# Four load buffers, earlier weights and row sums two ahead in a dilated convolution that runs at the pace of its transfers

## The chip, the cores and the metric

One core of a Trainium2 chip. The metric is the device time of one execution in microseconds (us). Runs marked slow are left out of every comparison, and the medians below are of the fast runs. A ratio is the mean time of one kernel's fast runs over the mean of the other's fast runs of the same rounds, so it isn't quite the ratio of the medians that are quoted. A span, where one is given, is the time from the first to the last instruction in the trace; the measured time is some 2 us longer. The granted clock is the share of its full clock at which TensorE was allowed to run.

## The reference

A 3x3 convolution with dilation 2, 64 channels in, 128 out, on 16 images of 64x64, all f32:

```python
batch, c_in, h, w, c_out, k, dilation = 16, 64, 64, 64, 128, 3, 2
x_pad = np.pad(x, ((0, 0), (0, 0), (pad, pad), (pad, pad)), mode='constant')
# for every b, co, ci, kh, kw:
output[b, co] += weight[co, ci, kh, kw] * x_pad[b, ci, kh*dilation:kh*dilation+h, kw*dilation:kw*dilation+w]
```

The input is 16.8 MB, the output 33.6 MB. Each byte is moved once: 50.63 MB with the weights.

## The kernel before

Images go in eight pairs (two images fill 128 partitions), each pair in four groups of 16 rows. ScalarE casts a group's rows to f16 (`cast`), VectorE adds pairs of rows (`rowsum`), TensorE multiplies into psP, psA and psB, ScalarE copies psP out (`p_sb`), and VectorE adds it to psA and psB while it evicts them (`evac`). The parts that matter here, with cuts:

```python
x32pool = ctx.enter_context(tc.tile_pool(name="x32pool", bufs=3))   # f32 pairs, filled by loads
xpool = ctx.enter_context(tc.tile_pool(name="xpool", bufs=3))       # f16 pairs, filled by casts
opool = ctx.enter_context(tc.tile_pool(name="opool", bufs=3))       # f32 output pairs
...
nc.sync.dma_start(out=w32, in_=weight.rearrange("o i h w -> o (i h w)"))
for pb in range(min(3, npairs)):
    load(pb, first[pb])
...
for i in range(14):                                     # dummies on TensorE
    nc.tensor.matmul(out=wp[:, 0:512], lhsT=warm[:, 0:P], rhs=warm)
...                                                     # weight differences wd
cast(0)
...
rowsum(0)
...                                                     # transposes wt, copies w_sb
def prepare(n):
    n = min(n, ngroups)
    while ahead[1] < min(n - 1 if n < ngroups else n, ahead[0]):
        rowsum(ahead[1]); ahead[1] += 1
    while ahead[0] < n:
        cast(ahead[0]); ahead[0] += 1

for G in range(ngroups):
    ...                                                 # products into psP, psA, psB; p_sb <- psP
    evac(0, psA)
    prepare(min(G + 3 + G // 3, G + 1 + LOOK))
    evac(1, psB)
    if ahead[0] >= NG * (freed[0] + 1) and freed[0] + 3 < npairs:
        load(freed[0] + 3, [H])                         # waits until the oldest f32 pair is cast
        freed[0] += 1
    ...                                                 # stores: pairs 0 and 7 in halves, others whole
```

Loads and stores are issued by SyncE, in this order, on one queue.

## Time and profile before

| | before |
|---|---|
| time, median of the first three runs | 133.54 us (132.32 to 134.15) |
| span of the profiled run (134.03 us) | 131.3 us |
| bytes moved | 50.63 MB |
| DMA rate where the queue is full | 428 GB/s |
| last eviction ends | 116.6 us |

The prediction below shows the lines. They are read from the DMA row: a digit is the busy share of the 16 DMA engines in a fortieth of the span, and the GB/s row tells whether busy engines also moved their bytes at the usual rate. A line of windows has, from left to right: from and to (us), the length, the busy us (and number of instructions) of TensorE, of its weight loads, of VectorE, ScalarE and GpSimd, then the granted clock, the DMA share and the GB/s. A DMA share near 1 means that all 16 engines are busy (it can read a little over 1, since a packet is counted where it starts).

The profiled run of 134.03 us is marked slow in its result file. Its span, 131.3 us, lies inside that of the fast runs of the same kernel (129.8 to 132.2), so the profile is used here.

### The profile page before, as it was taken

How to read it: one execution, taken by the hardware profiler on the slowest of the kernel's cores; microseconds unless marked ns; L12 is line 12 of the kernel's file. 1: busy time of each engine (PE TensorE's matmuls, PEld its weight loads, DVE VectorE, ACT ScalarE, POOL GpSimd, SP SyncE). 2: the span in 40 equal slices, each digit the busy share in tenths (PEclk: the TensorE clock that was granted, in tenths of full speed). 3: DMA queues.
4: the chain of work that ended last, by engine and by line, in shares of the span. 5: the costliest groups of instructions: out<-in, count | busy, mean ns of one | idle time of the engine just before them, and what ended most of it. 6: DMA issues, size and time to landing. Idle time of an engine off the chain costs nothing.

```text
span 131.3 us, 2313 instructions
## 1 busy us (share of the span) xinstructions
PE 107.2 (82%) x989; PEld 49.3 (38%) x989; DVE 89.9 (68%) x105; ACT 66.8 (51%) x71; POOL 0.7 (1%) x6
## 2 busy tenths in 40 slices
PE   6906898888999999999999999999999999900000
PEld 2502343333445444544444444444444544400000
DVE  0704466689788888988898889888888987750000
ACT  3536555474696766665565557666766433300000
POOL 2000000000000000000000000000000000000000
PEclk9996799999999999999999999999999999998555
DMA  5999938999999999999999999999999999999960
GB/s 165 399 424 439 424 160 274 359 397 419 429 432 334 369 299 434 424 412 444 424 439 424 422 429 429 434 429 419 429 434 434 414 434 429 429 419 417 429 284 17
DMA packets 4185, 50.76 MB, mean 387 GB/s; under 512 B 464, under 2 KB 464, under 8 KB 592
## 3 DMA queue, kind: packets, MB, share of 16 engines
q1 hardware_dynamic: 4176, 50.63, 93.4%
q8 instruction: 7, 0.11, 0.3%
q14 instruction: 2, 0.02, 0.0%
HBM read 17.07 MB, written 33.55 MB: 385 GB/s over the span
## 4 chain that ended last, share of the span: by engine, by line
PE 64%; DVE 2%; DVEq 1%; ACT 1%; issue 0%
PE psA L164 26%; PE psB L164 24%; PE psP L164 14%; DVE osb L220 2%; DVEq L270 1%; ACT x_266 L87 1%; DVE xs L97 0%; DVEq L220 0%
## 5 line engine op out<-in xcount | busy, mean ns | idle before, releaser
L164 PEld LDWEIGHTS <-w_sb 64*128 64x128 f16 x960 | 46.7, 95 | 61.6 <-DVE xs L97 4.7
L216 ACT COPY p_sb<-psP 128x1024 f32<-128x1024 f32 x32 | 32.4, 1013 | 40.3 <-issue 22.1
L220 DVE TENSOR_TENSOR osb<-psA,p_sb 128x1024 f32<-128x1024 f32 x32 | 39.2, 1225 | 19.2 <-PE psA L164 18.1
L220 DVE TENSOR_TENSOR osb<-psB,p_sb 128x1024 f32<-128x1024 f32 x32 | 39.0, 1218 | 0.0
L164 PE MATMUL psP<-xs,w_sb 64*128 64x496 f16 (+1 forms) x192 | 26.2, 379 | 6.8 <-DVE w_sb L150 4.3
L164 PE MATMUL psA<-x_117,w_sb 64*128 64x496 f16 (+3 forms) x48 | 6.7, 420 | 0.0
L87 ACT CAST x_117<-x_80 128x1024 f16<-128x1024 f32 (+2 forms) x4 | 4.2, 1054 | 3.3 <-DMA x_80<-in_x_dram 3.3
L122 PE MATMUL wp<-warm 128*128 128x512 f16 x14 | 4.7, 510 | 1.2 <-DVE warm L119 1.2
L164 PE MATMUL psB<-x_117,w_sb 64*128 64x496 f16 (+3 forms) x48 | 5.6, 366 | 0.0
L164 PE MATMUL psB<-x_266,w_sb 64*128 64x496 f16 (+3 forms) x48 | 5.6, 365 | 0.0
L164 PE MATMUL psB<-x_392,w_sb 64*128 64x496 f16 (+3 forms) x48 | 5.6, 365 | 0.0
L164 PE MATMUL psB<-x_681,w_sb 64*128 64x496 f16 (+3 forms) x48 | 5.6, 365 | 0.0
L164 PE MATMUL psB<-x_844,w_sb 64*128 64x496 f16 (+3 forms) x48 | 5.6, 365 | 0.0
L164 PE MATMUL psB<-x_518,w_sb 64*128 64x496 f16 (+3 forms) x48 | 5.6, 365 | 0.0
L164 PE MATMUL psB<-x_1166,w_sb 64*128 64x496 f16 (+3 forms) x48 | 5.6, 365 | 0.0
L164 PE MATMUL psA<-x_266,w_sb 64*128 64x496 f16 (+3 forms) x48 | 5.6, 365 | 0.0
L164 PE MATMUL psA<-x_392,w_sb 64*128 64x496 f16 (+3 forms) x48 | 5.6, 365 | 0.0
L164 PE MATMUL psA<-x_681,w_sb 64*128 64x496 f16 (+3 forms) x48 | 5.6, 365 | 0.0
L164 PE MATMUL psA<-x_844,w_sb 64*128 64x496 f16 (+3 forms) x48 | 5.6, 365 | 0.0
L164 PE MATMUL psB<-x_1005,w_sb 64*128 64x496 f16 (+3 forms) x48 | 5.6, 365 | 0.0
L164 PE MATMUL psA<-x_518,w_sb 64*128 64x496 f16 (+3 forms) x48 | 5.6, 365 | 0.0
L164 PE MATMUL psA<-x_1005,w_sb 64*128 64x496 f16 (+3 forms) x48 | 5.6, 365 | 0.0
(34 smaller groups left out, 60.6 us busy)
## 6 DMA issues: line engine op xcount, KB each, us to landing
out_dram<-osb SPq DMA_DIRECT2D x12, 2048.0 KB, 16.6
out_dram<-osb SPq DMA_DIRECT2D x8, 1024.0 KB, 11.1
x_80<-in_x_dram SPq DMA_DIRECT2D x1, 2048.0 KB, 7.6
x_82<-in_x_dram SPq DMA_DIRECT2D x1, 2048.0 KB, 12.0
x_84<-in_x_dram SPq DMA_DIRECT2D x1, 2048.0 KB, 16.5
x_225<-in_x_dram SPq DMA_DIRECT2D x1, 2048.0 KB, 8.5
x_353<-in_x_dram SPq DMA_DIRECT2D x1, 2048.0 KB, 13.0
x_476<-in_x_dram SPq DMA_DIRECT2D x1, 2048.0 KB, 10.6
```

The lines of the kernel that those rows point to most:

```text
L87: nc.scalar.copy(out=x16_tiles[pb][:, lo * W : hi * W], in_=x32_tiles[pb][:, lo * W : hi * W])
L122: nc.tensor.matmul(out=wp[:, 0:512], lhsT=warm[:, 0:P], rhs=warm)
L164: nc.tensor.matmul(out=po, lhsT=w_sb[pp, t * CO : (t + 1) * CO], rhs=rhs, start=first and j == 1, stop=last and j == 2,)
L216: nc.scalar.copy(out=p_sb, in_=psP)
L220: nc.vector.tensor_tensor(out=o[:, :, b0 : b0 + NBLK, e], in0=ps.rearrange("p (m b q) -> p m b q", m=2, q=2 * W), in1=pv, op=add,)
L270: with _tile.TileContext(nc) as tc:
```

## The change

The intent: keep the queue filled from the start (a fourth f32 buffer, paid for with the third f16 one), and let TensorE begin earlier and without gaps (weights ready before the first cast, dummies, products of zeros that nobody reads, so that its clock doesn't drop, row sums two groups ahead). The diff is abridged:

```diff
+    XB = 4
-    x32pool = ... bufs=3
-    xpool = ... bufs=3
+    x32pool = ... bufs=XB
+    xpool = ... bufs=2
-    for pb in range(min(3, npairs)):
-        load(pb, first[pb])
+    for pb in range(min(XB, npairs)):
+        load(pb, [H])
-    wp = apool.tile([P, 1024], f32, tag="ab", name="wp")
+    wp = ppool.tile([P, 1024], f32, tag="p", name="wp")
-    cast(0)
-    rowsum(0)                        (both ahead of the weights' transposes and copies)
+    run_warm(14)                     (14 more dummies, after them)
-    def prepare(n):                  (row sums first, one behind the casts)
+    def prepare(casts, sums):
+        while ahead[0] < min(casts, ngroups):
+            cast(ahead[0])
+            ahead[0] += 1
+        while ahead[1] < min(sums, ngroups):
+            rowsum(ahead[1])
+            ahead[1] += 1
-    prepare(2)
+    prepare(1, 1)
+    prepare(2, 2)
-        prepare(min(G + 3 + G // 3, G + 1 + LOOK))
+        prepare(min(G + 3 + (G + 1) // 2, G + 1 + LOOK), G + 3)
-        ... freed[0] + 3 < npairs: load(freed[0] + 3, [H])
+        ... freed[0] + XB < npairs: load(freed[0] + XB, [H])
```

More of the change, by code (lines that the diff above doesn't have):

```diff
@@ L53 @@
     chunk_rows = [(g * GR + (d if g else 0), min((g + 1) * GR + d, H)) for g in range(NG)]
+    XB = 4
     LOOK = 4
     wpool = ctx.enter_context(tc.tile_pool(name="wpool", bufs=1))
-    x32pool = ctx.enter_context(tc.tile_pool(name="x32pool", bufs=3))
-    xpool = ctx.enter_context(tc.tile_pool(name="xpool", bufs=3))
+    x32pool = ctx.enter_context(tc.tile_pool(name="x32pool", bufs=XB))
+    xpool = ctx.enter_context(tc.tile_pool(name="xpool", bufs=2))
     opool = ctx.enter_context(tc.tile_pool(name="opool", bufs=3))
@@ L109 @@
     nc.sync.dma_start(out=w32, in_=weight.rearrange("o i h w -> o (i h w)"))
-    first = [[H]] * 3
-    for pb in range(min(3, npairs)):
-        load(pb, first[pb])
+    for pb in range(min(XB, npairs)):
+        load(pb, [H])
     ident = wpool.tile([P, P], f16, name="ident")
@@ L119, with run_warm @@
     nc.vector.memset(warm, 0.0)
-    wp = apool.tile([P, 1024], f32, tag="ab", name="wp")
-    for i in range(14):
-        nc.tensor.matmul(out=wp[:, 0:512], lhsT=warm[:, 0:P], rhs=warm)
+    wp = ppool.tile([P, 1024], f32, tag="p", name="wp")
+    def run_warm(n):
+        for _ in range(n):
+            nc.tensor.matmul(out=wp[:, 0:512], lhsT=warm[:, 0:P], rhs=warm)
+    run_warm(14)
     KINDS = 5
@@ L134 @@
         nc.scalar.copy(out=wdv[:, 4, :, r], in_=wv[:, 2])
-    cast(0)
     for r in range(2):
         nc.vector.tensor_tensor(out=wdv[:, 3, :, r], in0=wv[:, 0], in1=wv[:, 1], op=sub)
-    rowsum(0)
     w_sb = wpool.tile([P, KINDS * KW * CO], f16, name="w_sb")
@@ L175, in blocks @@
         return lambda pp, c0, c1: v[pp, b0 : b0 + n, e, :, c0:c1]
-    ahead = [1, 1]
-    def prepare(n):
-        n = min(n, ngroups)
-        while ahead[1] < min(n - 1 if n < ngroups else n, ahead[0]):
+    run_warm(14)
+    ahead = [0, 0]
+    def prepare(casts, sums):
[3 more added lines that the diff above has]
+        while ahead[1] < min(sums, ngroups):
             rowsum(ahead[1])
             ahead[1] += 1
-        while ahead[0] < n:
-            cast(ahead[0])
-            ahead[0] += 1
-    prepare(2)
+    prepare(1, 1)
+    prepare(2, 2)
     freed = [0]
@@ L227 @@
         evac(0, psA)
-        prepare(min(G + 3 + G // 3, G + 1 + LOOK))
+        prepare(min(G + 3 + (G + 1) // 2, G + 1 + LOOK), G + 3)
         evac(1, psB)
-        if ahead[0] >= NG * (freed[0] + 1) and freed[0] + 3 < npairs:
-            load(freed[0] + 3, [H])
+        if ahead[0] >= NG * (freed[0] + 1) and freed[0] + XB < npairs:
+            load(freed[0] + XB, [H])
             freed[0] += 1
```

## The prediction

> **What bounds the kernel now.** I read the page's forty slices first, then the DMA queues, then windows cut where the DMA rows change, then the queue's own waits, and TensorE's timeline for the head. The slices:
>
> ```profile
> PE   6906898888999999999999999999999999900000
> DVE  0704466689788888988898889888888987750000
> PEclk9996799999999999999999999999999999998555
> DMA  5999938999999999999999999999999999999960
> GB/s 165 399 424 439 424 160 274 359 397 419 429 432 334 369 299 434 424 412 444 424 439 424 422 429 429 434 429 419 429 434 434 414 434 429 429 419 417 429 284 17
> ```
>
> TensorE has no work in the last five slices (16 us), VectorE in the last four; the DMA row stays at 9 almost to the end. The chain that ended last names TensorE for 64% of the span, but that chain only explains when the last store was issued: TensorE ends at 115.4 us of 131.3, and what remains is stores that were already queued. So the bound is the DMA queue, and what can be gained is the time in which it did not run at full rate. The windows show that time:
>
> ```profile
> 2.30:17.50 15.20, 10.39 (x69) 4.50 (x69) 6.51 (x12) 7.12 (x11) 0.00 (x0) 0.89 1.02 427
> 17.50:20.00 2.50, 2.26 (x22) 0.87 (x18) 1.40 (x2) 1.62 (x2) 0.00 (x0) 1.00 0.04 13
> 20.00:50.00 30.00, 28.25 (x270) 12.83 (x272) 24.21 (x29) 19.61 (x20) 0.00 (x0) 1.00 0.98 373
> 50.00:126.00 76.00, 65.22 (x634) 30.66 (x630) 57.55 (x63) 37.22 (x38) 0.00 (x0) 0.96 1.01 428
> 126.00:130.00 4.00, 0.00 (x0) 0.00 (x0) 0.00 (x0) 0.00 (x0) 0.00 (x0) 0.50 0.28 117
> ```
>
> The last two columns are DMA share and GB/s. Full rate here is 428 GB/s. There is one real hole, 17.5 to 20.0, and a stretch, 20 to 50, that runs at 373 although its share of busy time is 0.98: packets in it take longer. The last row is the tail, in which the 16 engines finish one after another.
>
> ```profile
> q1 hardware_dynamic: 4176, 50.63, 93.4%
> SPq L78 <- ACT x_117 L87: 10.3, 1, 10.3
> 11.08 1.43 PE L164 MATMUL psP<-xs,w_sb 64*128 64x512 f16 x6 [4.34 <-DVE w_sb L150]
> ...
> 16.42 0.81 PE L164 MATMUL psP<-xs,w_sb 64*128 64x512 f16 x6 [0.47 <-DVE xs L97]
> ```
>
> The first line is the page's (packets, MB, share), the second from the waits of the DMA queue, the others from TensorE's timeline (start, length). The second line gives the cause of the hole: the fourth load is held for 10.3 us until ScalarE has cast the last rows of the first pair (it is issued at 19.14), because there are three f32 buffers; the three loads in flight are done at 17.5, and the first store is not issued before 21.32. The other two show TensorE's head: it waits 4.34 us before its first product, and each of the next groups waits for its row sum.
>
> The time before as a sum of DMA terms: first bytes at 2.2; 50.63 MB at 428 GB/s is 118.3; hole 2.5 x 0.96 = 2.4; slow stretch 30 x (1 - 373/428) = 3.9; together 126.8, which is the mean end of the engines (126 + 4 x 0.28 = 127.1). The last engine is at about 129.9, a tail of 3.0, and the span closes 1.4 later. 2.2 + 118.3 + 2.4 + 3.9 + 3.1 + 1.4 = 131.3.
>
> **What the Trainium skill says.** "DMA: Bandwidth & Descriptors", section "Where 436 GB/s comes from", puts the ceiling of the SBUF side at 435 GB/s; 428 held for 76 us agrees, so the 118.3 us can't be shortened by any reordering. The same page, "Queues, rings and completion order", says that each engine consumes its ring in order; so a load queued behind another starts with no gap, and the trace agrees (the three first loads run at 427 without a dip). "TensorE: Matmul & The Clock Gate", section "Part 1: The HAM clock gate", says that an idle window of about 3.4 us halves the clock; the trace agrees: TensorE idles 4.34 us, the granted clock is then 0.78 and 0.50 in the two windows from 10 to 14 us, and the first 12 products of psA take 2.38 us instead of 1.27.
>
> **The change part by part.**
>
> *Four f32 buffers.* The head has four loads queued at once instead of three, 0.29 + 4 x 2.10 = 8.68 MB, which takes until 2.2 + 20.3 = 22.5 us. The first store (21.3 in the old order, earlier in the new) and the fifth load (its buffer is free after the last cast of pair 0, about 17 us) are both queued before that. The hole of 2.4 us goes. I also expect most of the 3.9 us of the slow stretch to go, with less certainty. Inside it the dips lie at 20 to 22 and 24.5 to 27, and at 41 to 43 and 45 to 48: around the loads issued at 19.14 and 40.58, which are exactly the two that found the queue empty. The loads at 30.59, 52.95 and 65.32, which found stores ahead of them, run without a dip. In the changed kernel every load finds a backlog. Left over: 0.5.
>
> *Two f16 buffers instead of three.* They make room. A cast at four groups ahead needs the pair two before to be finished; in program order it follows the copy of the present group's psP, by which time TensorE has left that pair. Cost: 0.
>
> *Weights before casts, 14 more dummies.* The weight copies (two of 0.58 on VectorE, two of 0.53 on ScalarE) move from behind the first cast into ScalarE's idle time before the load lands at 8.8; the first product then waits only for cast (1.15) and row sum (0.43): 8.81 + 1.15 + 0.43 + 0.1 = 10.5 instead of 11.08. The dummies, 14 x 0.22 = 3.0 us, fill 6.7 to 9.8, so that TensorE idles under 1 us and keeps its clock.
>
> *Row sums two ahead.* The first six groups start at 11.08, 16.42, 20.22, 24.02, 27.82 and 31.47, the seventh at 34.65: 23.6 us for six, where the steady pace is 12.36 for four, or 3.09 each. At 3.1 to 3.2 they take 18.8, so TensorE gains 4.8 + 0.6 = 5.4 us and ends near 110. VectorE has 2 x 1.22 + 0.42 = 2.86 per group and ScalarE 1.01 + 1.05, both under 3.09; in odd groups of the head ScalarE has two casts, 3.1 in all, which just fits.
>
> *The queue replayed.* With groups of 3.09 from 10.5, stores are issued at about 18.2 and 24.4 (pair 0), then 36.7, 49.1, 61.5, 73.9, 86.2, 98.6, and 104.8 and 110.9 for the last pair. A load takes 4.9, a pair's stores 9.8. In issue order the queue is filled until 22.5, 27.4, 32.3, 37.2, 42.1, 47.0, 56.8, 61.7, 71.5, 81.3, 91.1, 100.9, 110.7, 115.6, 120.5. Each issue comes before the queue has run dry; the tightest is 98.6 against 100.9. The output buffers (three pairs) come free in time too: pair 5 wants one at 74.4, and the stores of pair 2 have landed by about 73.5. So the bound stays with the DMA queue and the head of TensorE only makes sure of it.
>
> Sum: 2.2 + 118.3 + 0.0 (hole) + 0.5 (slow packets) + 1.9 (tail, less than 3.1 since fewer slow packets put the engines out of step) + 1.4 = 124.3 us of span. The profiled run took 134.03 with a span of 131.3, so 2.7 more: 127.0 us, 5% less than 133.54.
>
> **The rivals.** *The slow packets stay.* If they belong to loads that run beside stores and not to loads that find the queue empty, up to 3.9 us stays and the tail stays at 3: span 128.8, time 131.5, within 2%. Against it: 50 to 126 holds two such loads at 428. *TensorE or the output buffers become the bound.* If row sums or casts still hold TensorE and it ends at 113 rather than 110, the stores of pair 6 come at 101.6 against 100.9, a hole of about 2 us with the issue latency: 129. For it: only 2.3 us of margin; against it: the sums per group above. *Only one part works.* Either part alone would already close the first hole: earlier casts issue the fourth load at about 17, the fourth buffer needs none. The gains do not add; whoever adds 2.4 + 3.9 + 5.4 would say 122, which the byte count forbids: 2.2 + 118.3 + 1.4 + 2.7 = 124.6 is the least.
>
> **Range and chances.** Low 125.2 is that least plus half a microsecond of tail. High 130.0 is the prediction with the old tail (1.2) and nearly half of the slow packets (1.8). The runs before lie within 1.4% of each other, so faster than 130.87 has 0.93, the same 0.065, slower 0.005: no part adds work on the queue.
>
> **What would show it.** DMA share 9 from the second slice on, no slice under 400 GB/s before the tail; the span's mean near 407 GB/s; the first product near 10.5 with a full clock after it; TensorE's wait for row sums gone; first stores issued near 18.5, stores of the second pair near 36.7, TensorE's end near 110. Slow packets with a full queue, or a wait of VectorE for the output buffers that leads to a hole in the queue, would prove it wrong.

## The result, and the profile after

127.87 us in the median of three fast runs (127.62 to 127.88), against 133.54 for the kernel before; with every run counted the medians are 127.88 and 133.84. The ratio of the fast runs is 0.9584 (95% interval 0.9475 to 0.9693). A fourth took 659.4 us; it is left out, and nothing here explains it. It did not come back in ten more runs of the same kernel.

The slices of the changed kernel, the same rows as before:

```profile
PE   6999999999999999999999999999999999900000
DVE  0732888898888888888988879889888988740000
PEclk9999999999999999999999999999999999995555
DMA  5899999999999999999999999999999999999960
GB/s 171 370 447 437 416 416 432 453 291 406 445 434 403 442 439 427 434 416 421 432 437 419 426 421 427 442 432 427 426 421 432 432 421 432 426 408 432 424 278 23
```

TensorE is busy from the second slice on, by the clock row its clock is full until it has nothing left to do, and the DMA row has no hole. (The clock row doesn't show the start: the first 14 dummies took 0.43 us each, the 14 added ones 0.23.) One slice is out of line: the ninth, 291 GB/s at a busy share of 9. That was not foreseen. The windows, with the DMA share and GB/s in the last two columns:

```profile
2.20:22.50 20.30, 20.24 (x152) 10.06 (x151) 12.39 (x19) 12.83 (x17) 0.00 (x0) 1.00 1.01 423
22.50:50.00 27.50, 27.50 (x273) 15.19 (x269) 24.10 (x27) 18.20 (x19) 0.00 (x0) 1.00 1.01 415
50.00:120.00 70.00, 60.28 (x585) 32.85 (x580) 53.25 (x59) 34.51 (x36) 0.00 (x0) 0.95 1.01 427
120.00:122.00 2.00, 0.00 (x0) 0.00 (x0) 0.00 (x0) 0.00 (x0) 0.00 (x0) 0.50 0.78 328
122.00:126.00 4.00, 0.00 (x0) 0.00 (x0) 0.00 (x0) 0.00 (x0) 0.00 (x0) 0.50 0.10 43
```

The mean end of the DMA engines is 120 + 2 x 0.78 + 4 x 0.10 = 122.0 us, where it was 127.1: that is 5.1 of the 5.3 us by which the span fell (131.3 to 126.0). So the time came out of the queue: 2.4 us of hole, and 2.8 us of slow packets (3.9 before, 1.1 now, see below). The queue's share of the span and the head of the chain that ended last:

```profile
q1 hardware_dynamic: 4176, 50.63, 95.7%
...
PE 86%; DVE 1%; DVEq 1%; issue 0%
```

The chain puts 86% on TensorE now, more than before (64%), because TensorE no longer pauses; it still is only the way to the issue of the last store. The queue's issues and the head of TensorE, from the timeline (start, length, what):

```profile
11.14 0.81 PE L166 MATMUL psP<-xs,w_sb 64*128 64x512 f16 x6
14.16 0.81 PE L166 MATMUL psP<-xs,w_sb 64*128 64x512 f16 x6
16.88 0.34 SPq L79 DMA_DIRECT2D x_245<-in_x_dram  x1
17.33 0.81 PE L166 MATMUL psP<-xs,w_sb 64*128 64x512 f16 x6
19.06 0.82 SPq L101 DMA_DIRECT2D out_dram<-osb  x2
```

Groups now start 3.02 and 3.17 us apart where they started 5.34 and 3.80 apart. The fifth load (x_245) is issued at 16.88 and the first stores at 19.06, both while the four loads of the head still run (till about 22.5).

### The profile page after: what moved, and what is told of

It reads as the page before. It is cut to its first block, busy times and chain, and to the rows that moved or that the text cites. A ratio compares the mean times of both kernels' runs of the same rounds, so it can differ in the third digit from the quotient of the medians.

```text
span 126.0 us, 2342 instructions
## 1 busy us (share of the span) xinstructions
PE 109.0 (87%) x1003; PEld 58.5 (46%) x1003; DVE 90.0 (71%) x105; ACT 66.8 (53%) x71; POOL 0.7 (1%) x6
## 3 DMA queue, kind: packets, MB, share of 16 engines
q1 hardware_dynamic: 4176, 50.63, 95.7%
## 4 chain that ended last, share of the span: by engine, by line
PE 86%; DVE 1%; DVEq 1%; issue 0%
PE psA L166 31%; PE psB L166 30%; PE psP L166 16%; PE wp L124 7%; DVE osb L223 1%; DVEq L273 1%; PE wt L146 1%; DVE warm L119 0%; DVEq L223 0%
## 5 line engine op out<-in xcount | busy, mean ns | idle before, releaser
L166 PEld LDWEIGHTS <-w_sb 64*128 64x128 f16 x960 | 54.3, 94 | 45.0 <-DVE xs L98 0.5
L124 PE MATMUL wp<-warm 128*128 128x512 f16 x28 | 9.2, 502 | 1.2 <-DVE warm L119 1.2
L124 PEld LDWEIGHTS <-warm 128*128 128x128 f16 x28 | 3.3, 121 | 5.9 <-issue 3.3
L166 PE MATMUL psA<-x_369,w_sb 64*128 64x496 f16 (+3 forms) x48 | 5.6, 365 | 0.0
L166 PE MATMUL psA<-x_532,w_sb 64*128 64x496 f16 (+3 forms) x48 | 5.6, 365 | 0.0
L166 PE MATMUL psA<-x_695,w_sb 64*128 64x496 f16 (+3 forms) x48 | 5.6, 365 | 0.0
L166 PE MATMUL psA<-x_1017,w_sb 64*128 64x496 f16 (+3 forms) x48 | 5.6, 365 | 0.0
L166 PE MATMUL psA<-x_157,w_sb 64*128 64x496 f16 (+3 forms) x48 | 5.6, 365 | 0.0
L166 PE MATMUL psA<-x_240,w_sb 64*128 64x496 f16 (+3 forms) x48 | 5.6, 365 | 0.0
L166 PE MATMUL psA<-x_856,w_sb 64*128 64x496 f16 (+3 forms) x48 | 5.6, 365 | 0.0
L166 PE MATMUL psB<-x_157,w_sb 64*128 64x496 f16 (+3 forms) x48 | 5.6, 365 | 0.0
L166 PE MATMUL psB<-x_369,w_sb 64*128 64x496 f16 (+3 forms) x48 | 5.6, 365 | 0.0
L166 PE MATMUL psB<-x_532,w_sb 64*128 64x496 f16 (+3 forms) x48 | 5.6, 365 | 0.0
L166 PE MATMUL psB<-x_1017,w_sb 64*128 64x496 f16 (+3 forms) x48 | 5.6, 365 | 0.0
L166 PE MATMUL psB<-x_1178,w_sb 64*128 64x496 f16 (+3 forms) x48 | 5.6, 365 | 0.0
L166 PE MATMUL psB<-x_695,w_sb 64*128 64x496 f16 (+3 forms) x48 | 5.6, 365 | 0.0
L166 PE MATMUL psB<-x_856,w_sb 64*128 64x496 f16 (+3 forms) x48 | 5.6, 365 | 0.0
L166 PE MATMUL psA<-x_1178,w_sb 64*128 64x496 f16 (+3 forms) x48 | 5.6, 365 | 0.0
```

The source lines that it names most:

```text
L166: nc.tensor.matmul(out=po, lhsT=w_sb[pp, t * CO : (t + 1) * CO], rhs=rhs, start=first and j == 1, stop=last and j == 2,)
```

## The experiments

All results are correct. "Changed" is the changed kernel, run again in the first and third group of runs; the kernel before was run beside each group (medians 132.84, 132.80 and 133.09).

| run | median us | ratio to before | last eviction starts |
|---|---|---|---|
| changed, first group | 128.04 | 0.9639 | 109.83 |
| four buffers only | 128.62 | 0.9677 | 115.23 |
| head only, three f32 buffers | 128.54 | 0.9668 | 109.99 |
| stores ahead of loads | 127.76 | 0.9613 | 110.33 |
| no added dummies | 127.89 | 0.9637 | 111.77 |
| row sums and casts as before | 128.23 | 0.9655 | 113.33 |
| 2.1 MB more loaded | 133.53 | 1.0048 | 111.19 |
| loads of x on ScalarE's queue | 130.10 | 0.9803 | 115.86 |
| all loads on ScalarE's queue | 127.40 | 0.9580 | 111.00 |
| stores first and no added dummies | 128.61 | 0.9659 | 112.84 |
| changed, third group | 127.86 | 0.9614 | 109.99 |

**Is the queue the bound?** More bytes, nothing else:

```diff
+    extra = wpool.tile([P, 1024], f32, name="extra")
...
+        if G in (8, 14, 20, 26):
+            nc.sync.dma_start(out=extra, in_=x_pair[0, :, 0:1024])
```

> The changed kernel with four more loads of 0.52 MB each, 2.1 MB in all, into a buffer that nobody reads, at groups 8, 14, 20 and 26; the result stays correct. Theory (the bytes on the queue set the time): 2.1 MB at 428 GB/s is 4.9 us more, 132.5 to 133.3 us, with TensorE ending within 1 us of where it ended. Rival (TensorE or the evictions set it, the queue has room): under 2 us more.

It took 133.53 us. By the ratios to the kernel before (1.0048 against 0.9639 and 0.9614 of the changed kernel) that is 5.4 to 5.8 us more for 2.1 MB, while the last eviction started 0.8 to 1.4 us later than in the three profiles of the changed kernel (110.42, 109.83, 109.99). The queue's line of that run (packets, MB, share), beside 4176, 50.63 and 95.7% of the changed kernel:

```profile
q1 hardware_dynamic: 4752, 52.73, 96.0%
```

The queue is the bound. The 0.5 to 0.9 us above 4.9 weren't pursued; these rows are 4 KB long where the others have 8 or 16.

**Which part did it?** The kernel before with the buffers alone:

```diff
-    x32pool bufs=3, xpool bufs=3, first = [[H]] * 3, min(3, npairs), freed[0] + 3
+    x32pool bufs=4, xpool bufs=2, first = [[H]] * 4, min(4, npairs), freed[0] + 4
```

> The kernel before with four f32 and two f16 pair buffers and nothing else of the change. Theory (the queue is the bound, and TensorE's head only decides when stores arrive): the hole at 17.5 us goes, but the groups still start at 11.1 with five late row sums, so the last stores are issued at about 117 us as before and the queue runs dry before the stores of pairs 5 and 6 arrive (91 and 101 us by the replay against issues at about 92 and 104): new holes of 3 to 5 us in sum between 90 and 110 us. Span about 129, time about 131 us, 2 to 3 us over the full change. Rival (the buffers are what counts): no late hole, time within 0.7 us of the full change, about 128.

And the changed kernel without them:

```diff
-    XB = 4
-    xpool ... bufs=2
+    XB = 3
+    xpool ... bufs=3
```

> The full change with three f32 and three f16 pair buffers: only weights first, dummies and row sums ahead. Theory: the fourth load is issued at about 17 us as its buffer comes free earlier, the hole shrinks from 2.5 us to under 1 us, and the rest is as in the full change: time 0.3 to 1 us over it, 128.2 to 128.9 us. Rival (the fourth buffer is what counts): the hole stays at 2 us or more and the slow packets at both ends of the fourth load too, time above 130 us.

> The changed kernel unaltered, beside its parts on the same chip: 127.9 us as before, span about 126.0, the slow packets at 25.7 to 28 us again at the same place.

128.62 and 128.54 us, beside 128.04 for both parts and 132.84 for none. So each part alone has over four fifths of the gain (4.2 and 4.3 of 4.8 us), and they don't add; by the intervals of the ratios, what the second part brings on top isn't clear of noise. The changed kernel again had its slow packets at 26 to 28 us (279 GB/s). Head only: the early casts issue the fourth load earlier, and the hole becomes a dip:

```profile
18.00:20.00 2.00, 2.00 (x22) 0.95 (x20) 1.52 (x2) 1.75 (x2) 0.00 (x0) 1.00 0.78 270
```

A second dip follows at 22 to 24 us (238 GB/s), just ahead of the first stores.

Buffers only: the late hole that the theory asked for is there, and something that it had not asked for. Windows of that kernel:

```profile
102.00:106.00 4.00, 4.00 (x46) 1.95 (x42) 3.85 (x5) 1.29 (x2) 0.00 (x0) 1.00 0.60 250
...
120.00:122.00 2.00, 0.00 (x0) 0.00 (x0) 0.00 (x0) 0.00 (x0) 0.00 (x0) 0.50 0.97 406
122.00:126.00 4.00, 0.00 (x0) 0.00 (x0) 0.00 (x0) 0.00 (x0) 0.00 (x0) 0.50 0.78 326
```

The changed kernel has 426 GB/s in the first of these windows. The hole is 4 x 0.40 = 1.6 us, not 3 to 5. And the engines' mean end is 122 + 4 x 0.78 = 125.1 us, 3.1 later than in the changed kernel (122.0), but the span is only 1.1 us longer (127.1). The rest was given back in the tail: in the changed kernel the engines finish between 120 and some 124.5 us, here all are still busy from 122 to 124 (a window of its own gives 1.05) and none after 126. I read it so: an engine that is behind has packets left when the others run dry, so a hole costs the early engines time and the late ones little, and it is the latest that sets the time. The packet records of the trace bear this out, though they don't name the engine. At full rate 16 packets are under way. In this run the number falls to 8 at 103.25 us, 2 at 104.25 and 1 at 105.25, and is 16 again at 105.5: the engines ran dry one after another and started again together. At the end all 16 run until about 125.1 and the last packet ends at 125.6; in the changed kernel the number falls from 121 on and the last ends at 124.5. My expectation of 131 us had charged the hole to the mean.

**The smaller parts.** Without the added dummies:

```diff
-    run_warm(14)
     ahead = [0, 0]
```

> The changed kernel without the 14 added dummies. Theory (queue bound, TensorE has a margin): TensorE idles over 3 us ahead of its first product, the granted clock falls to about 0.5 to 0.8 between 10 and 14 us, the first group takes about 2 us longer and TensorE ends near 112 instead of 110; the stores of pair 6 are then issued about when the queue would run dry, so the time stays within 0.6 us of the changed kernel, 127.7 to 128.5 us. Rival (each microsecond of the head counts): 2 us more, about 130 us.

127.89 us. Granted clock (third column from the right) from 10 to 14 us, first in the changed kernel, then without the dummies:

```profile
10.00:14.00 4.00, 3.94 (x36) 2.00 (x35) 1.67 (x3) 3.46 (x4) 0.00 (x0) 1.00 0.97 414
```

```profile
10.00:14.00 4.00, 2.87 (x16) 1.09 (x18) 0.85 (x2) 2.95 (x4) 0.00 (x0) 0.57 1.03 442
```

The dummies do what they are meant to do, TensorE gains 1.3 us or more by them (last eviction at 110.42 or earlier against 111.77), and by itself none of it reaches the time.

With row sums and casts in the order of before:

```diff
-    def prepare(casts, sums): ...        prepare(1, 1); prepare(2, 2)
+    cast(0); rowsum(0); def prepare(n): (as in the kernel before)   prepare(2)
-        prepare(min(G + 3 + (G + 1) // 2, G + 1 + LOOK), G + 3)
+        prepare(min(G + 3 + G // 3, G + 1 + LOOK))
```

> The changed kernel with the row sums and casts in the order of before (one sum ahead, issued ahead of the casts); weights first, dummies and buffers as changed. Theory: TensorE waits again for row sums in the first groups, about 4 us in all, and ends near 113 to 114 us; the stores of pair 6 come 1 to 2 us after the queue has run dry, a hole of about 1 us near 100 us, partly given back in the tail: 128.2 to 129 us. Rival: 4 us more, about 132 us.

128.23 us: TensorE's weight loads wait 5.2 us for row sums again (0.5 in the changed kernel), the last eviction is some 3 us later (113.33), and a small hole opens:

```profile
102.00:104.00 2.00, 2.00 (x24) 1.00 (x22) 1.85 (x3) 0.55 (x1) 0.00 (x0) 1.00 0.58 246
122.00:126.00 4.00, 0.00 (x0) 0.00 (x0) 0.00 (x0) 0.00 (x0) 0.00 (x0) 0.50 0.35 145
```

2 x 0.42 = 0.8 us of hole, and again most of it comes back in the tail: the mean end is 122 + 4 x 0.35 = 123.4, 1.4 us later, and the span 0.5 us longer (126.5). By its interval (0.9602 to 0.9709) this is not clear of the changed kernel.

**The slow packets at 26 us.** In the changed kernel the fifth load was queued behind others, and its last packets were slow all the same. They lie just ahead of the first stores. To move the first switch from loads to stores:

```diff
-        if ahead[0] >= NG * (freed[0] + 1) ...: load(...); freed[0] += 1
         if pb in (0, npairs - 1) and g % 2 == 1: store(...)
         elif 0 < pb < npairs - 1 and g == NG - 1: store(...)
+        if ahead[0] >= NG * (freed[0] + 1) ...: load(...); freed[0] += 1
```

> The changed kernel with each load issued after the stores of its group and not ahead of them, so that the first stores follow the fourth load directly. Theory A (load packets slow down when all engines go from loads to stores in step, the first such switch): the slow packets move to the end of the fourth load, about 20.5 to 22.5 us, and the fifth load, which now comes between stores, has none. Theory B (it belongs to the fifth load itself or to that moment, 26 us): they stay with the fifth load or at 26 us. The time is 127.9 within 0.4 us under A, up to 0.9 us less if no load is slow.

Windows of the changed kernel, then of this one:

```profile
22.00:24.00 2.00, 2.00 (x24) 1.18 (x22) 1.52 (x3) 2.00 (x3) 0.00 (x0) 1.00 1.07 459
24.00:26.00 2.00, 2.00 (x24) 1.18 (x22) 1.83 (x3) 1.79 (x3) 0.00 (x0) 1.00 1.04 426
26.00:28.00 2.00, 2.00 (x22) 1.03 (x19) 2.00 (x3) 1.05 (x2) 0.00 (x0) 1.00 0.99 262
```

```profile
22.00:24.00 2.00, 2.00 (x24) 1.15 (x21) 1.52 (x3) 2.00 (x3) 0.00 (x0) 1.00 0.68 238
24.00:26.00 2.00, 2.00 (x24) 1.14 (x20) 1.83 (x3) 1.78 (x3) 0.00 (x0) 1.00 1.02 430
26.00:28.00 2.00, 2.00 (x22) 1.11 (x20) 2.00 (x3) 1.05 (x2) 0.00 (x0) 1.00 1.00 422
```

The dip moved from 26 to 22 us, to the end of the fourth load, and the fifth has none. (The share of 0.68 isn't a hole, since a window counts a packet where it starts: by the packet records 15.6 to 16 packets were under way all the time, and one took 2.1 us where 0.61 is usual.) So it goes with a switch from loads to stores and not with a load or a moment. It need not be the first switch: with the buffers only there is a dip at 26 us and another at 46 to 48 (303 GB/s at a share of 1.00), ahead of the second pair's stores, and the last run below has its dip ahead of the second stores and none ahead of the first. Why one switch is slow and another isn't, the runs don't say; that it needs all engines in step remains a guess. The time, 127.76 us, is the same as of the changed kernel: the dip only moved.

Mixing the packets of loads and stores, by a second queue, was to spread the switch:

```diff
-            nc.sync.dma_start(out=t[:, lo * W : hi * W], in_=x_pair[pb, :, lo * W : hi * W])
+            nc.scalar.dma_start(out=t[:, lo * W : hi * W], in_=x_pair[pb, :, lo * W : hi * W])
```

> The changed kernel with the loads of x issued by ScalarE on its own queue, stores and weights on the other. [...]Theory A (load packets slow down where all engines go from loads to stores in step): with the first stores mixed in among the loads the switch is spread out; slow packets fall below 0.5 us per engine or spread over 18 to 30 us, and the time is 127.0 to 128.0 us. Rival (any load packet beside a store is slow): many more slow packets, under 400 GB/s over 20 to 60 us, and 129 us or more. The issue costs ScalarE about 0.4 us per load, which it has.

130.10 us, and this is a miss for a reason that neither theory had: the weights, now alone on the other queue, no longer come ahead of x. VectorE waits 7.3 us for them where it waited 2.5, TensorE's first product starts at 16.59, and the queue runs dry later:

```profile
102.00:106.00 4.00, 4.00 (x45) 2.28 (x41) 3.50 (x4) 1.92 (x3) 0.00 (x0) 1.00 0.55 225
```

The run says nothing on mixing. With the weights on the same queue as x, ahead of it:

> As the run with the loads of x on ScalarE's queue, but with the weights on that queue too, ahead of x. In that run the weights, alone on the other queue, arrived about 5 us late, TensorE began at 16.6 us and the queue ran dry near 104 us, which hid what mixing does. Now the weights land as in the changed kernel, TensorE begins within 1.5 us of it, and there is no late hole. If mixing spreads the switch (theory A), the window with under 300 GB/s between 18 and 30 us is gone and the time is 127.0 to 127.8 us; if a load packet beside stores is slow anyway, such a window stays and the time is 128 us or more.

127.40 us (127.39 to 127.53, four runs) against 127.86 (127.59 to 128.10, six runs) of the changed kernel on the same chip. Its slowest window:

```profile
22.00:24.00 2.00, 2.00 (x24) 1.16 (x21) 1.52 (x3) 2.00 (x3) 0.00 (x0) 1.00 0.85 340
```

The dip is softer, not gone. This is the fastest version, by some 0.4 us; the two sets of runs don't overlap, though the intervals of their ratios do (0.9539 to 0.9621 and 0.9576 to 0.9651). That the softer dip is the reason isn't shown.

> The changed kernel unaltered on this chip, for the comparison with the two others: 127.6 to 128.4 us.

That is the 127.86 us above.

Last, the two edits that had cost nothing alone, together (stores ahead of loads, no added dummies):

> Stores ahead of loads and without the added dummies, both of which cost nothing alone: the candidate for a leaner kernel. Theory (queue bound): 127.7 to 128.1 us, the same as the changed kernel; TensorE ends 1.4 us later than there. A gain of over 0.4 us would say that the dummies' instructions cost the queue something.

128.61 us (127.71 to 129.53, six runs), 0.7 us more than the changed kernel. By the medians that is a miss, but the runs scatter and the intervals of the ratios overlap (0.9611 to 0.9708 and 0.9576 to 0.9651), so it isn't clear of noise. Three runs with a mean granted clock of 0.928 to 0.930 took 128.62 to 129.53, the three with 0.949 to 0.955 took 127.71 to 128.61. The profile is of the slowest: TensorE stays at half its clock beyond 16 us, the first stores are issued at 21.49, not 18.97 (stores ahead of loads alone), and the stretch from 22.5 to 50 us runs at 392 GB/s instead of 415 (changed). Its first switch to stores comes at 22.5 us, its second at 34:

```profile
22.00:24.00 2.00, 2.00 (x24) 0.87 (x20) 2.00 (x3) 0.79 (x2) 0.00 (x0) 1.00 0.93 385
32.00:34.00 2.00, 2.00 (x22) 0.88 (x20) 1.83 (x3) 0.98 (x2) 0.00 (x0) 1.00 0.80 213
```

It may be that two edits that cost nothing alone cost something together, since each uses up some of the same margin; this run doesn't show it. Which of its runs had how many dips isn't known.

## Why the prediction was right, and where it wasn't

The time was predicted as 127.0 us (125.2 to 130.0) and came to 127.88. The steps:

- **The bound** (the DMA queue): right, and shown by the added bytes, 5.4 to 5.8 us for 2.1 MB.
- **The hole at 17.5 us**: gone, as said.
- **"Either part alone would already close the first hole"**: right; the parts alone gave 4.2 and 4.3 of 4.8 us.
- **TensorE's head**: nearly right. The first product starts at 11.14, not 10.5: its 14 first dummies took 6.04 us instead of 4.71 in this run, so that everything behind them came later: the weights' copies on ScalarE held up the first cast by 0.6 us (9.40 instead of 8.81), the first row sum ended at 11.02 and the added dummies at 11.09. In the third group's profile of the same kernel it starts at 10.62. Row sums hold TensorE no longer, and its end (last psB evicted at 111.6) is 5.0 us earlier, where 5.4 was said.
- **Slow packets, 0.5 us left over**: mis-sized. The step that failed is "in the changed kernel every load finds a backlog", taken as enough for full rate. By the windows 20.3 x (1 - 423/428) + 27.5 x (1 - 415/428) = 0.2 + 0.8 = 1.1 us remained, most of it at the first switch from loads to stores, behind a full queue (a sign that the prediction had itself named as one against it). With the buffers only, a load that had a backlog was slow too (46 to 48 us). Since the cause of the slow packets is open, 2.8 of the 5.1 us are measured and not explained.
- **The tail, 1.9 us**: mis-sized. The mean end is 122.0 and the last packet ends at 124.5 us, so it is about 2.5 us, hardly shorter than before (127.1 to 129.9). I had put it down to slow packets; it stayed when most of them went. It is short, about 0.5 us, in the kernel with the buffers only, where the late hole let the engines start together.
- **The 2.7 us between span and time**: mis-sized the other way. I had one pair to take it from, a run that is marked slow. In the fast runs of the kernel before in the three groups it lies between 1.7 and 2.8, and in the changed kernel's runs between 1.7 and 1.9.

So the span was predicted 1.7 us short (124.3 against 126.0) and the constant 0.8 us long, and the two errors partly cancelled. The rival with all slow packets left (131.5) was wrong. Of the rival in which TensorE or the output buffers become the bound, the late hole is real as soon as TensorE ends 3 us later (row sums as before), but it cost 0.2 to 0.4 us of the time (128.23 against 127.86 and 128.04) where 2 us were set against it.

## What to carry to other kernels

Where a queue is full to the end, count its bytes first: their time at the measured full rate is the floor, and every proposed gain in another engine is worth only the hole that it closes. Two changes that fill the same hole don't add, and once it is filled, further speed of the engines that feed the queue is margin. A hole is felt by each DMA engine on its own: where they finish spread over several us, a short hole costs less than its length, since it takes the time mostly from those that are early (here a mean of 1.6 us, while one packet or more was always under way).

## What the Trainium skill lacked or had wrong

- "DMA: Bandwidth & Descriptors", section "Where 436 GB/s comes from", says that for transfers between HBM and SBUF the HBM side binds at about 358 GB/s. Here one core that worked alone moved 427 GB/s, loads and stores together, for 70 us. The passage doesn't say that its figure leaves this case out; other passages of the skill do.
- No page has the slow load packets ahead of a switch from loads to stores: 262 GB/s for 2 us at a busy share of 0.99, moved by 4 us when the first stores were put one load earlier (238 GB/s), and in one profile ahead of the second stores instead (213 GB/s).
- "DMA: Bandwidth & Descriptors", section "Issuing engines are not separate DMA queues", says that issuing from several engines saves only issue time. Loads on one queue and stores on the other gave 127.40 us against 127.86, too little to contradict it. What the section leaves out is the harm: one small load that stood alone on the second queue came some 5 us later (VectorE waited 7.3 us for it instead of 2.5).
- "TensorE: Matmul & The Clock Gate", section "Part 1: The HAM clock gate", gives the idle window after which the clock is halved as about 3.4 us. Without the added dummies TensorE idled 3.01 us and the granted clock still fell: in windows of 1 us it is 1.00 from 9 to 10 us, 0.76 from 10 to 11 and 0.50 from 11 to 12, so that it fell some 2.4 us after TensorE's last product had ended at 8.12.
- No page gives the size of the spread in which the 16 engines of one queue finish (mean end 122.0 us, last packet 124.5), or says that a hole in the queue takes the spread away (all ended between 125.1 and 125.6 us with the buffers only).
